# Two chained transformer blocks: context loads and their norm moved within the start, a root fewer in one norm, the last product in column halves

## The chip, the cores and the metric

The kernel runs on one core of a Trainium2 chip. The metric is the device time of one execution in microseconds (us); the time before is a median of three runs. The engines are called TensorE (PE in the rows; PEld is its weight loading), VectorE (DVE), ScalarE (ACT), GpSimd (POOL) and SyncE (SP). SP issues every DMA of this kernel, in one queue.

## The reference, cut to what matters

All tensors are float32. `x` is 256 tokens of 1024 features; `ctx` and `mem` are 256 tokens each. Two blocks run one after the other, depth 1 each.

```
mod   = silu(c) @ w_ada + b_ada;   mod_c = silu(c_ctx) @ w_ada + b_ada     # 6 x 1024 each
h  = rms(x,   g_norm1) * (1 + sc1)  + sh1        # "modulation"
hc = rms(ctx, g_norm1) * (1 + scc1) + shc1
... = split(h @ w_in);  ... = split(hc @ w_in)   # latent attention + retention, both with rotary angles
x  = x + gt1 * ([o_mla, o_ret] @ w_out)
x  = x + gt2 * conv_ffn(rms(x, g_norm2) * (1 + sc2) + sh2)
x  = rms(x, g_final)                             # end of block 1
u  = rms(x, g_mix_pre)                           # start of block 2
z  = u @ w_in_2  -> qa ka va | qh fh ih gh
ya = sliding-window attention(qa, ka, va);  yh = rms(hgrn2(qh, fh, ih), g) * silu(gh)
x  = x + rms([ya, yh] @ w_out_2, g_mix_post)
x  = x + rms(cross_attention(rms(x), rms(mem) @ wk, rms(mem) @ wv) @ wo, g_x_post)
x  = x + rms((silu(u @ w_gate) * (u @ w_up)) @ w_down, g_ffn_post)     # w_down is 2816 x 1024
```

Every rms divides by sqrt(mean of squares + 1e-6).

## The kernel before, in words

Every large product is made of three matmuls (`mm3`, L183): each operand is split into a rounded high part and a low part, and high times high, high times low and low times high are summed in PSUM. A weight arrives as a raw tile of 128 x 1024 (512 KB, one DMA); seven such tiles circulate. ACT writes the high part (L219, or L224 with a gain), DVE the low part (L220, L225), into one of four pairs, more from block 1's feed-forward on. A raw tile is free for the next DMA when its last reader is done.

The program is written as one sequence, and a planner puts it in order: it takes each instruction's place in the text as its priority (a helper with `prio` gets a place some instructions further ahead: 20 for `norm_T`), reckons times with costs of its own, and gives an idle engine the ready instruction of the best place. What comes out is one fixed order for each engine's queue, and an engine works its queue strictly in that order. An instruction far down the text may therefore stand early in a queue.

**The start** is driven by a string, `START`, one letter for each step. `m` is one of 16 steps of the memory's keys and values (`mem_steps`: `k_step` for `wk_x`, `v_step` for `wv_x`; L397 and L183), which need nothing of the modulation; `a` loads one of 16 tiles of `w_ada` and multiplies it straight from the raw tile (`ada_unit`, DMA at L329, matmuls at L331); `x` and `c` load `x` and `ctx` transposed (two DMAs of 512 KB each, L305); `k` loads the rotary constants (258 KB, L450); `X` and `C` call `norm_T` on the one or the other. `norm_T` squares on ACT (L360), adds on DVE (L362 to L365), sums over features with two matmuls against a column of ones (L368), takes the root on POOL (L136, L137), spreads it with a matmul (L375, L377) and multiplies the tile (L430). After the last `a`, `ada_fm` turns the two sums into columns (copy L336, transposes L343, L346, L350), `mod_split` modulates `x` on ACT and DVE (L471, L474) and splits it (L157, L158), and the memory steps that are left follow (L483). Then comes the first product of block 1 (`proj`, the retention's queries), in whose course `mod_split` runs for `ctx`, and the product for the latent attention's inputs, the first to read `ctx`.

**Block 2** works the two halves of the tokens (`seg2(0)` and `seg2(1)`) as generators, one some steps behind the other. At its head (L1352 to L1375) block 1's last residual is added, `xr` and `gx = xr * g_final` are squared and summed on ACT (L141), and POOL makes two scalars for each token: `r1`, the root of the final norm, and `r`, that of both norms together. ACT then scales `gx` by `r1` (L1375), and each product of `w_in_2` is scaled by `r` when it leaves PSUM (L1395). `hgrn2` (L1150 to L1208) ends with its own norm: ACT squares the output `o` (L1199), DVE multiplies `o` by the gate (L1201) and reduces the squares (L1203), POOL takes the root, DVE multiplies by it (L1206), and PE transposes the result (`transpose_split`, L165).

**The end** (L1470 to L1472) is the last six rows of tiles of `w_down`, six units for each half of the tokens; each unit multiplies into two PSUM tiles of 512 columns. `post_norm` follows for each half: squares on ACT (L141), gain on DVE (L1090), root on POOL (L145, L146), scaled addition on DVE (L1095), DMAs out.

Of the kernel before, what the change touches and what calls it, by code (L numbers as in the profile page):

```python
# [14 lines left out]
ALU = mybir.AluOpType  # L15
AX = mybir.AxisListType
# [4 lines left out]
D = 1024  # L21
KD = D // P
FF = 2816
KF = FF // P
EPS = 1e-6
# [5 lines left out]
MLA_ACT = (2, 5)  # L31
MOD = 'VVAVVAVA'
MID = 1
START = 'mmaamxXmaammaammaamaamaakmaaacaC'
NT2 = 5
NS1 = 4
ZORD = ('ka', 'qa', 'qh', 'gh', 'fh', 'ih')
# [50 lines left out]
def _body(nc, tc, A, out, es):  # L88
# [202 lines left out]
    with ExitStack() as e1:  # L291
# [133 lines left out]
        @prio("nt")  # L425
        def norm_T(dst):
            r, rb = token_rms(dst)
            for q in range(2):
                ks = slice(4 * q, 4 * q + 4)
                nc.vector.tensor_tensor(out=dst[:, ks, :], in0=dst[:, ks, :],  # L430
                                        in1=rb.unsqueeze(1).broadcast_to([P, 4, T]), op=ALU.mult)

        n_mem = n_ada = 0
        for ch in START:
            if ch == "m":
                mem_steps[n_mem]()
                n_mem += 1
                if n_mem == 2:
                    mem_norm()
            elif ch == "a":  # L440
                ada_unit(1 - n_ada % 2, n_ada // 2, ada0[1 - n_ada % 2])
                n_ada += 1
            elif ch == "x":
                for q in range(2):
                    load_T(xnT, "xT", q)
            elif ch == "c":
                for q in range(2):
                    load_T(cnT, "ctxT", q)
            elif ch == "k":
                nc.sync.dma_start(c1, A["cst1"][:, 128:NC1])  # L450
            elif ch == "X":
                norm_T(xnT)
            elif ch == "C":
                norm_T(cnT)
        while n_ada < 16:
            ada_unit(1 - n_ada % 2, n_ada // 2, ada0[1 - n_ada % 2])
            n_ada += 1
# [22 lines left out]
            return X  # L480

        hx = mod_split(xnT, sh1[:, 0:8], sc1[:, 0:8])
        for i in range(n_mem, 16):  # L483
            mem_steps[i]()

        rdec = cp.tile([P, 8], F32, name="rdec")
        bc_row(rdec, "ret_decay")
# [514 lines left out]
        split_from(hh[:, 0:nb, :], hl[:, 0:nb, :], ya[:, 0:nb, :])  # L1002
        return hh, hl

    def ffn_down(u, t, hT, accs):
        k = u.ks[0]
        hh, hl = hT[k // 4]
        sl = slice(t * P, (t + 1) * P)
        wh, wl = u.get()
        mm3(accs, hh[:, k % 4, sl], hl[:, k % 4, sl], [wh[:, 0:512], wh[:, 512:1024]],  # L1010
            [wl[:, 0:512], wl[:, 512:1024]], k == 0, k == KF - 1)

    wdown_units = units_for(W, A["w_down"], 0, 1024, KF)
    bcs = {}
# [134 lines left out]
    @prio("h2")  # L1149
    def hgrn2(t, ih, parts, gate):  # L1150
        qs, ks, qi, kd, decs = parts
        Sst = once("state", state)[0]
        at = at_tile()
        for h in range(4):
            for c in range(2):
                cols = slice(h * P + 64 * c, h * P + 64 * c + 64)
                nc.tensor.matmul(at[64 * c:64 * c + 64, cols], lhsT=ks[:, cols], rhs=qs[:, cols], start=True, stop=True)
        for c in range(2):
            cs = slice(64 * c, 64 * c + 64)
            blocks = lambda a: a[cs, :].rearrange("p (h c n) -> p h c n", h=4, c=2)[:, :, c, :]  # L1160
            nc.vector.copy_predicated(blocks(ATs), C2("causal")[cs, cs].bitcast(U32).unsqueeze(1).broadcast_to([64, 4, 64]),
                                      blocks(at))
        tt = tr_tile()
        for h in range(4):
            hs = slice(h * P, (h + 1) * P)
            nc.tensor.transpose(tt[:, hs], kd[:, hs], ident)
        kdT, yh = pair()
        nc.scalar.copy(kdT, tt)
        nc_ = 2 - t
        kvs = [at_tile() for _ in range(nc_)]  # L1170
        for h in range(4):
            hs = slice(h * P, (h + 1) * P)
            for c in range(nc_):
                nc.tensor.matmul(kvs[c][:, hs], lhsT=kdT[64 * c:64 * c + 64, hs], rhs=ih[64 * c:64 * c + 64, hs],
                                 start=True, stop=True)
        for c in range(nc_):
            cg = 2 * t + c
            if cg == 0:
                nc.scalar.copy(Sst[0], kvs[c])
            else:  # L1180
                for h in range(4):
                    hs = slice(h * P, (h + 1) * P)
                    nc.vector.scalar_tensor_tensor(out=Sst[cg][:, hs], in0=Sst[cg - 1][:, hs],
                                                   scalar=decs[:, 2 * h + c:2 * h + c + 1], in1=kvs[c][:, hs],
                                                   op0=ALU.mult, op1=ALU.add)
        o = at_tile()
        for h in range(4):
            hs = slice(h * P, (h + 1) * P)
            for c in range(2):
                cs = slice(64 * c, 64 * c + 64)  # L1190
                nc.tensor.matmul(o[cs, hs], lhsT=ATs[cs, h * P + 64 * c:h * P + 64 * c + 64], rhs=ih[cs, hs],
                                 start=True, stop=2 * t + c == 0)
            for c in range(2):
                cg = 2 * t + c
                if cg:
                    nc.tensor.matmul(o[64 * c:64 * c + 64, hs], lhsT=qi[:, h * P + 64 * c:h * P + 64 * c + 64],
                                     rhs=Sst[cg - 1][:, hs], start=False, stop=True)
        sq = S2()
        nc.scalar.activation(sq, o, AF.Square, scale=128.0 ** -0.5)  # L1199
        if gate is not None:  # L1200
            nc.vector.tensor_tensor(out=yh, in0=o, in1=gate, op=ALU.mult)  # L1201
        ss = small(4, "hss")
        nc.vector.tensor_reduce(out=ss, in_=sq.rearrange("p (h n) -> p h n", h=4), axis=AX.X, op=ALU.add)  # L1203
        r = finish_rstd(ss, 4)
        src = o if gate is None else yh
        nc.vector.tensor_tensor(out=yh.rearrange("p (h n) -> p h n", h=4), in0=src.rearrange("p (h n) -> p h n", h=4),  # L1206
                                in1=r.unsqueeze(2).broadcast_to([P, 4, P]), op=ALU.mult)
        return yh  # L1208
# [137 lines left out]
    def seg2(t):  # L1346
# [17 lines left out]
        for i in range(2):  # L1364
            c = slice(i * 512, (i + 1) * 512)
            nc.vector.tensor_tensor(out=gx[:, c], in0=xr[t][:, c], in1=g[:, c], op=ALU.mult)
            mean_sq(xr[t][:, c], D, ss[0][:, i:i + 1])
            mean_sq(gx[:, c], D, ss[1][:, i:i + 1])
        r1 = rstd2(ss[0])
        r = small(1, "rf")  # L1370
        nc.gpsimd.tensor_tensor(out=r, in0=r1, in1=r1, op=ALU.mult)
        nc.gpsimd.tensor_scalar(out=r, in0=ss[1][:, 0:1], scalar1=ss[1][:, 1:2], scalar2=r, op0=ALU.add, op1=ALU.mult)
        r = finish_rstd(r)
        nc.gpsimd.tensor_tensor(out=r, in0=r, in1=r1, op=ALU.mult)
        nc.scalar.activation(xr[t], gx, AF.Copy, scale=r1)  # L1375
        yield
        Z, zs = {}, []
# [90 lines left out]
                for t in range(2):  # L1468
                    ffn_down(u, t, hT2, dacc[t])
    for t in range(2):  # L1470
        for u in down[16:]:
            ffn_down(u, t, hT2, dacc[t])  # L1472
        post_norm(t, dacc[t], "g_ffn_post", True)


# [83 lines left out]
```

## Time and profile before

| | |
|---|---|
| median of 3 runs | 839.96 us (839.39 to 840.77) |
| profiled execution | 838.46 us, its span 836.7 us |
| mean granted clock of TensorE | 0.992 of full speed |
| busy: PE, PEld, DVE, ACT, POOL | 804.2, 652.2, 618.8, 481.1, 40.7 us |
| DMA | 155.20 MB, 186 GB/s over the span |

Times in rows count from the start of the span. In a timeline, the bracket behind an instruction tells how long its engine stood idle before it and what it waited for. In a table of stretches, each engine's busy time stands with its number of instructions, and the last three columns are the granted clock of TensorE, the busy share of the DMA engines and GB/s.

### The profile page before, as it was taken

The numbers are of one execution on the slowest core, as the hardware profiler recorded it, in microseconds if no ns is written. First come the engines' busy times: TensorE is split into PE (matmuls) and PEld (weight loads), VectorE is DVE, ScalarE is ACT, GpSimd is POOL, SyncE is SP. The second block draws the span as 40 slices with busy tenths as digits, with TensorE's granted clock in tenths as the row PEclk, the third lists the DMA queues.
The fourth block names the chain that finished last, engine by engine and source line by source line (L and its number), as shares of the span: only waits on it lengthen the run. The fifth ranks groups of instructions, "written<-read, shape, count | busy, mean of one in ns | idle before, by whom it ended". The sixth has DMA issues, their size and how long they took to land.

```text
span 836.7 us, 11995 instructions
## 1 busy us (share of the span) xinstructions
PE 804.2 (96%) x4384; PEld 652.2 (78%) x4384; DVE 618.8 (74%) x1043; ACT 481.1 (58%) x850; POOL 40.7 (5%) x76
## 2 busy tenths in 40 slices
PE   5989999999999999999999999999999999999996
PEld 4757978776787888888887777767888788888885
DVE  5739889996787698878868656786747887867743
ACT  7338364334655685656656656565626876756631
POOL 0000010000010200000001300001001100000000
PEclk9999999999999999999999999999999999999999
DMA  9797889872166557566564453343624576566501
GB/s 336 262 359 267 268 288 327 280 232 78 49 186 186 180 186 226 179 200 198 181 177 153 134 166 127 126 130 121 201 76 121 173 240 197 178 200 195 184 1 51
DMA packets 81531, 155.20 MB, mean 186 GB/s; under 512 B 5184, under 2 KB 43584, under 8 KB 81472
## 3 DMA queue, kind: packets, MB, share of 16 engines
q1 hardware_dynamic: 81472, 154.44, 57.4%
q8 instruction: 34, 0.56, 0.3%
q14 instruction: 25, 0.20, 0.1%
HBM read 152.85 MB, written 1.05 MB: 184 GB/s over the span
## 4 chain that ended last, share of the span: by engine, by line
PE 77%; ACT 3%; DVE 2%; POOL 2%; issue 2%; POOLq 0%; DVEq 0%; ACTq 0%
PE acc L183 38%; PE tr L250 9%; PE at L250 7%; PE tr L253 4%; PE at L253 4%; PE at L746 2%; PE tr L768 1%; PE at L183 1%; ACT junk L141 1%; PE tr L165 1%; PE at L1326 1%; PE tr L757 1%; PE at L1304 1%; PE at L718 1%; POOL rs L137 1%
## 5 line engine op out<-in xcount | busy, mean ns | idle before, releaser
L183 PE MATMUL acc<-wh,xT 128*128 128x512 f32 (+2 forms) x544 | 169.3, 388 | 1.8 <-ACT xT L157 1.8
L219 ACT CAST wh<-raw 128x1024 fp32r<-128x1024 f32 (+1 forms) x90 | 91.1, 1012 | 84.1 <-PE acc L183 31.1
L220 DVE TENSOR_TENSOR wl<-raw,wh 128x1024 fp32r<-128x1024 f32 (+1 forms) x90 | 105.6, 1176 | 40.2 <-ACT wh L219 40.0
L183 PEld LDWEIGHTS acc<-wh,xT 128*128 128x128 f32 x544 | 98.4, 189 | 24.6 <-issue 4.1
L220 DVE TENSOR_TENSOR xl<-raw,xh 128x1024 fp32r<-128x1024 f32 x68 | 82.6, 1220 | 29.8 <-ACT xh L219 29.6
L183 PE MATMUL acc<-wl,xT 128*128 128x512 f32 (+2 forms) x272 | 98.4, 387 | 0.0
L224 ACT ACTIVATE wh<-raw,fm 128x256 fp32r<-128x256 f32 (+3 forms) x128 | 70.4, 605 | 44.4 <-DMA raw<-in_wv_x_dram 15.6
L183 PE MATMUL acc<-xh,xT 128*128 128x512 f32 x288 | 92.8, 397 | 0.0
L219 ACT CAST xh<-raw 128x1024 fp32r<-128x1024 f32 x68 | 70.9, 1047 | 35.7 <-PE acc L183 12.1
L225 DVE SCALAR_TENSOR_TENSOR wl<-raw,fm,wh 128x256 fp32r<-128x256 f32 (+3 forms) x128 | 71.8, 609 | 17.3 <-ACT wh L224 17.1
L183 PEld LDWEIGHTS acc<-xh,xT 128*128 128x128 f32 x288 | 53.6, 189 | 11.6 <-issue 0.7
L250 PE MATMUL tr<-xT,wh 128*128 128x512 f32 x192 | 61.2, 398 | 0.0
L183 PEld LDWEIGHTS acc<-wl,xT 128*128 128x128 f32 x272 | 50.3, 189 | 10.3 <-issue 2.5
L183 PE MATMUL acc<-xl,xT 128*128 128x512 f32 x144 | 53.5, 399 | 0.1
L225 DVE SCALAR_TENSOR_TENSOR xl<-raw,fm,xh 128x256 fp32r<-128x256 f32 (+2 forms) x76 | 38.0, 551 | 14.6 <-ACT xh L224 14.6
L224 ACT ACTIVATE xh<-raw,fm 128x256 fp32r<-128x256 f32 (+2 forms) x76 | 37.7, 559 | 18.5 <-PE acc L183 9.8
L183 PE MATMUL acc<-xh,g 128*128 128x512 f32 x160 | 44.1, 389 | 0.0
L253 PEld LDWEIGHTS tr<-xT,wl 128*128 128x128 f32 x192 | 36.1, 188 | 7.9
L250 PE MATMUL at<-xT,xh 128*128 128x512 f32 x128 | 40.2, 395 | 0.0
L250 PE MATMUL at<-xT,wh 128*128 128x512 f32 x128 | 40.2, 395 | 0.0
L250 PE MATMUL tr<-xT,xh 128*128 128x512 f32 x128 | 40.2, 395 | 0.0
L253 PE MATMUL tr<-xT,wl 128*128 128x256 f32 x192 | 38.6, 278 | 0.0
(366 smaller groups left out, 1544.5 us busy)
## 6 DMA issues: line engine op xcount, KB each, us to landing
raw<-in_w_up_dram SPq DMA_DIRECT2D x66, 512.0 KB, 4.3
raw<-in_w_ada_dram SPq DMA_DIRECT2D x48, 512.0 KB, 5.6
raw<-in_w_down_dram SPq DMA_DIRECT2D x44, 512.0 KB, 4.3
raw<-in_w_in_dram SPq DMA_DIRECT2D x38, 512.0 KB, 4.6
raw<-in_w_gate_dram SPq DMA_DIRECT2D x22, 512.0 KB, 4.7
raw<-in_w_out_dram SPq DMA_DIRECT2D x16, 512.0 KB, 3.6
raw<-in_wk_x_dram SPq DMA_DIRECT2D x8, 512.0 KB, 6.0
raw<-in_wv_x_dram SPq DMA_DIRECT2D x8, 512.0 KB, 8.6
```

Of the source, the lines that this page charges most:

```text
L137: nc.gpsimd.tensor_tensor(out=r, in0=r, in1=mhalf[:, 0:w], op=ALU.pow)
L141: nc.scalar.activation(junk[:, 0:a.shape[-1]], a, AF.Square, scale=n ** -0.5, accum_out=ss)
L165: nc.tensor.transpose(t[:, j * P:(j + 1) * P], src[:, (b + j) * P:(b + j + 1) * P], ident)
L183: nc.tensor.matmul(accs[i], lhsT=xl if f == 2 else xh, rhs=wl[i] if f == 1 else wh[i], start=first and f == 0, stop=last and f == 2)
L219: nc.scalar.copy(wh[:, 0:n], raw[:, 0:n])
L220: nc.vector.tensor_tensor(out=wl[:, 0:n], in0=raw[:, 0:n], in1=wh[:, 0:n].bitcast(F32), op=ALU.subtract)
L224: nc.scalar.activation(wh[:, s], raw[:, s], AF.Copy, scale=gains[k])
L225: nc.vector.scalar_tensor_tensor(out=wl[:, s], in0=raw[:, s], scalar=gains[k], in1=wh[:, s].bitcast(F32), op0=ALU.mult, op1=ALU.subtract)
L250: nc.tensor.matmul(a, lhsT=wh[:, o + b * P:o + (b + 1) * P], rhs=both, start=k == 0, stop=False, skip_group_check=True)
L253: nc.tensor.matmul(a[:, T:2 * T], lhsT=wl[:, o + b * P:o + (b + 1) * P], rhs=X.h[:, k, :], start=False, stop=k == 7, skip_group_check=True)
L718: nc.tensor.matmul(a, lhsT=wt[:, j * P:(j + 1) * P], rhs=xt[:, k, :], start=n == 0, stop=n == 5)
L746: nc.tensor.matmul(sc, lhsT=qTa[0:96, h, ts_], rhs=kTa[h // 4][0:96, h % 4, :], start=True, stop=True)
```

## The change

Four places are changed. In the start, the loads of `ctx` and of the rotary constants come earlier in the string, between memory steps: `ctx` goes from behind the 15th `w_ada` tile to behind the 6th, the constants from behind the 12th to behind the 8th. The norm of `ctx` leaves the string and goes behind the modulation of `x` and one more memory step. In `hgrn2` the reduction of the squares is put ahead of the product with the gate. At the head of block 2 the seven POOL instructions become five: `r1` keeps the sum of squares, `r` is a root of one sum, and the product of two roots is gone; the squares of `gx` come behind both squares of `xr`. At the end, the second half of the tokens does all six units for the left 512 columns and then all six for the right ones.

```diff
-START = 'mmaamxXmaammaammaamaamaakmaaacaC'
+START = 'mmaamxXmaammaacmmaakmaamaamaaaa'
+REST = 'mCmmmm'
...
-            elif ch == "C":
-                norm_T(cnT)
...
         hx = mod_split(xnT, sh1[:, 0:8], sc1[:, 0:8])
-        for i in range(n_mem, 16):
-            mem_steps[i]()
+        for ch in REST:
+            if ch == "m":
+                mem_steps[n_mem]()
+                n_mem += 1
+            elif ch == "C":
+                norm_T(cnT)
...
-    def ffn_down(u, t, hT, accs):
+    def ffn_down(u, t, hT, accs, part=(0, 1)):
...
-        mm3(accs, hh[:, k % 4, sl], hl[:, k % 4, sl], [wh[:, 0:512], wh[:, 512:1024]],
-            [wl[:, 0:512], wl[:, 512:1024]], k == 0, k == KF - 1)
+        cols = [slice(512 * i, 512 * i + 512) for i in part]
+        mm3([accs[i] for i in part], hh[:, k % 4, sl], hl[:, k % 4, sl], [wh[:, c] for c in cols],
+            [wl[:, c] for c in cols], k == 0, k == KF - 1)
...
         nc.scalar.activation(sq, o, AF.Square, scale=128.0 ** -0.5)
+        ss = small(4, "hss")
+        red = nc.vector.tensor_reduce(out=ss, in_=sq.rearrange("p (h n) -> p h n", h=4), axis=AX.X, op=ALU.add)
         if gate is not None:
-            nc.vector.tensor_tensor(out=yh, in0=o, in1=gate, op=ALU.mult)
-        ss = small(4, "hss")
-        nc.vector.tensor_reduce(out=ss, in_=sq.rearrange("p (h n) -> p h n", h=4), axis=AX.X, op=ALU.add)
+            with tc.issue_after(red.ins):
+                nc.vector.tensor_tensor(out=yh, in0=o, in1=gate, op=ALU.mult)
...
             mean_sq(xr[t][:, c], D, ss[0][:, i:i + 1])
-            mean_sq(gx[:, c], D, ss[1][:, i:i + 1])
-        r1 = rstd2(ss[0])
+        for i in range(2):
+            mean_sq(gx[:, i * 512:(i + 1) * 512], D, ss[1][:, i:i + 1])
+        r1 = small(1, "rg")
         r = small(1, "rf")
-        nc.gpsimd.tensor_tensor(out=r, in0=r1, in1=r1, op=ALU.mult)
-        nc.gpsimd.tensor_scalar(out=r, in0=ss[1][:, 0:1], scalar1=ss[1][:, 1:2], scalar2=r, op0=ALU.add, op1=ALU.mult)
-        r = finish_rstd(r)
-        nc.gpsimd.tensor_tensor(out=r, in0=r, in1=r1, op=ALU.mult)
+        e = small(1, "ef")
+        nc.gpsimd.tensor_scalar(out=r1, in0=ss[0][:, 0:1], scalar1=ss[0][:, 1:2], scalar2=EPS, op0=ALU.add, op1=ALU.add)
+        nc.gpsimd.tensor_scalar(out=e, in0=r1, scalar1=EPS, scalar2=None, op0=ALU.mult)
+        nc.gpsimd.tensor_scalar(out=r, in0=ss[1][:, 0:1], scalar1=ss[1][:, 1:2], scalar2=e, op0=ALU.add, op1=ALU.add)
+        nc.gpsimd.tensor_tensor(out=r, in0=r, in1=mhalf[:, 0:1], op=ALU.pow)
+        nc.gpsimd.tensor_tensor(out=r1, in0=r1, in1=mhalf[:, 0:1], op=ALU.pow)
...
-        for u in down[16:]:
-            ffn_down(u, t, hT2, dacc[t])
+        for part in ((0, 1),) if t == 0 else ((0,), (1,)):
+            for u in down[16:]:
+                ffn_down(u, t, hT2, dacc[t], part)
```

`issue_after` keeps the product behind the reduction in DVE's queue.

## Rows read from the trace of the kernel before

**Rows 1.** The page's first part: busy us, share of the span, instructions

```profile
PE 804.2 (96%) x4384; PEld 652.2 (78%) x4384; DVE 618.8 (74%) x1043; ACT 481.1 (58%) x850; POOL 40.7 (5%) x76
```

**Rows 2.** Stretches of the start: length, busy us by engine, clock, DMA share, GB/s

```profile
24.00:32.00 8.00, 6.73 (x54) 4.96 (x54) 6.41 (x12) 2.10 (x4) 0.96 (x2) 1.00 0.61 196
36.00:56.00 20.00, 20.00 (x164) 14.74 (x166) 5.53 (x8) 4.01 (x6) 0.00 (x0) 1.00 0.95 332
58.00:66.00 8.00, 6.05 (x22) 3.54 (x23) 4.87 (x9) 4.07 (x8) 1.38 (x2) 0.57 1.04 376
72.00:88.00 16.00, 16.00 (x72) 13.17 (x71) 15.92 (x26) 12.51 (x19) 0.00 (x0) 1.00 0.92 306
88.00:111.00 23.00, 23.00 (x170) 22.26 (x169) 18.93 (x24) 7.97 (x12) 0.00 (x0) 1.00 0.86 297
```

**Rows 3.** Timeline of PE from 58 to 65 us: start, us, instruction, idle before

```profile
58.96 1.08 PE L331 MATMUL at<-raw,silc 128*32 128x256 f32 x8 [2.25 <-DMA raw<-in_w_ada_dram]
...
60.86 1.01 PE L368 MATMUL tr<-ones,s1k 128*128 128x1 f32 x4 [0.82 <-DVE s1k L365]
...
64.19 1.22 PE L377 MATMUL tr<-s1k,ones 128*128 128x256 f32 x2 [0.17 <-DVE s1k L375]
```

**Rows 4.** Timeline of SP's queue in the start

```profile
48.79 0.90 SPq L305 DMA_DIRECT2D s<-in_ctxT_dram  x2
49.78 0.60 SPq L329 DMA_DIRECT2D raw<-in_w_ada_dram  x1
51.92 5.86 SPq L209 DMA_DIRECT2D raw<-in_wv_x_dram  x5
```

**Rows 5.** Timeline of ACT around 57 to 61 us

```profile
57.31 1.06 ACT L360 ACTIVATE g<-s 128x1024 f32<-128x1024 f32 x1 [0.23 <-DMA s<-in_ctxT_dram]
60.47 1.33 ACT L224 ACTIVATE wh<-raw,fm 128x512 fp32r<-128x512 f32 x2 [2.11 <-DMA raw<-in_wv_x_dram]
```

**Rows 6.** All waits of PE: waiting line, releaser, us, times, longest

```profile
PE tr L165 <- DVE g L1206: 2.5, 2, 1.7
...
PE acc L183 <- DVE wl L225: 1.3, 2, 0.8
```

**Rows 7.** Timeline of DVE at 6 us

```profile
5.73 0.16 DVE L1063 TENSOR_TENSOR lmx<-fm 128x4 f32<-128x4 f32 x1 [4.44 <-DMA fm<-in_fm_dram]
```

**Rows 8.** Groups of DVE from 56 to 93 us: count, busy us, mean ns

```profile
L430 DVE TENSOR_TENSOR s<-s,tr 128x1024 f32<-128x1024 f32 x2 | 2.4, 1218 | 0.7 <-PE tr L377 0.7
L362 DVE TENSOR_TENSOR g<-g,g 128x1024 f32<-128x1024 f32 x1 | 1.2, 1226 | 6.2 <-ACT g L360 6.2
```

**Rows 9.** Timeline of DVE in the second half's hgrn2

```profile
565.49 0.69 DVE L1201 TENSOR_TENSOR g<-at,g 128x512 f32<-128x512 f32 x1 [1.47 <-ACT t L1199]
```

**Rows 10.** Two more stretches: behind hgrn2's second norm, and one with short stalls

```profile
570.00:576.00 6.00, 6.00 (x24) 4.75 (x23) 4.63 (x6) 3.60 (x8) 0.87 (x2) 0.72 0.26 87
112.00:117.50 5.50, 3.48 (x16) 1.67 (x15) 3.19 (x14) 4.37 (x17) 2.80 (x6) 1.00 0.89 349
```

**Rows 11.** Timeline of POOL at block 2's head, first and second half of tokens

```profile
459.17 2.49 POOL L1371 TENSOR_TENSOR rf<-rs 128x1 f32<-128x1 f32 x1
...
467.84 0.19 POOL L1371 TENSOR_TENSOR rf<-rs 128x1 f32<-128x1 f32 x1
```

**Rows 12.** Timeline of DVE in the same stretch

```profile
459.79 1.22 DVE L220 TENSOR_TENSOR wl<-raw,wh 128x1024 fp32r<-128x1024 f32 x1
```

**Rows 13.** Timeline of ACT in the same stretch

```profile
459.13 1.16 ACT L1375 ACTIVATE xr<-g,rs 128x1024 f32<-128x1024 f32 x1 [0.77 <-POOL rs L146]
...
464.86 0.48 ACT L1395 ACTIVATE g<-acc,rs 128x256 f32<-128x256 f32 x1 [3.97 <-POOL rs L1374]
```

**Rows 14.** Timeline of PE in the same stretch

```profile
467.81 0.39 PE L183 MATMUL acc<-wh,xT 128*128 128x256 f32 x1 [1.23 <-ACT xT L157]
```

**Rows 15.** Timeline of ACT and PE at the end

```profile
829.22 0.39 PE L183 MATMUL acc<-wh,g 128*128 128x512 f32 x1
...
829.75 0.60 ACT L141 ACTIVATE junk<-acc 128x512 bf16<-128x512 f32 x1
```

More of the change, by code (lines that the diff above doesn't have):

```diff
@@ L482, in _body @@
         hx = mod_split(xnT, sh1[:, 0:8], sc1[:, 0:8])
-        for i in range(n_mem, 16):
-            mem_steps[i]()
+        for ch in REST:
[4 more added lines that the diff above has]
+                norm_T(cnT)
+        assert n_mem == 16
         rdec = cp.tile([P, 8], F32, name="rdec")
```

## The prediction

> **What bounds the kernel now.** The page's first part comes first: PE is busy for 804.2 us of the span, far ahead of DVE's 618.8 [rows 1]. A gain can therefore come from two places only: time in which PE stands still, and time in which it works at the lower of its two clocks. The table of stretches shows where the start loses both. From 36 to 56 us PE is busy for 20.00 of 20.00 us while DVE does 5.53; from 58 to 66 us the granted clock is 0.57, so that most of the stretch runs at 1.2 GHz instead of 2.4; from 72 to 88 us PE and DVE are both full (16.00 and 15.92 of 16.00 us) [rows 2]. PE's timeline then says what stood ahead of the slow stretch: PE waits 2.25 us for the last tile of `w_ada`, then 0.82 us for DVE's sum of ctx's squares, then 0.17 us for ctx's spread root [rows 3]. SP's queue shows why that tile is late: ctx's two loads are issued right ahead of it, at 48.79 us, the tile itself at 49.78, and the DMA engines are 95% busy from 36 to 56 us [rows 2, 4]. Last, the list of PE's waits: of what is behind the start, the wait of hgrn2's transpose for DVE (2.5 us in two waits, the longer 1.7) is touched by the change, and the 1.3 us for low parts of weights may be [rows 6].
>
> **The start.** Removed from the queue ahead of the last w_ada tile are two loads of 512 KB, 1.05 MB; at the 376 GB/s of the slow stretch they take 2.8 us [rows 2, 4]. They don't vanish: ctx now goes ahead of five weight tiles and nine tiles of w_ada, and the constants (258 KB) ahead of two weight tiles and four of w_ada. From 24 to 32 us the DMA engines are busy for 0.61 of the time [rows 2]; the free 3.1 us hold 1.17 MB at 376 GB/s. So ctx fits in and 0.14 MB of the constants are left over, 0.4 us, for the tiles behind. I cost that at nothing, because PE is full from 36 to 56 us and its next tile is there when it asks; without that cover it is the 0.4 us. The first reader of the constants comes far behind their old place.
>
> The last w_ada tile lands 2.8 us sooner, which covers the 2.25 us of waiting. The two waits for ctx's norm (0.82 and 0.17) lie ahead of the first transposes of the modulation and go with the norm: 3.24 us in all [rows 3]. What is late next is the weight of the twelfth memory step: ACT begins its high part at 60.47 us, when its DMA lands [rows 5]. It is behind the same 1.05 MB, so about 57.7; half of ACT's 1.33 us later PE can begin, 58.4. PE is through with the last w_ada tile at 58.96 - 2.25 = 56.7 and half of the row's 1.08 us at the full clock, 57.3 [rows 3]. A new wait of 1.1 us stands in place of the old 3.24.
>
> The clock: 6.05 us of work at 0.57 cost 6.05 x 0.43 = 2.6 us [rows 2]. It fell behind a wait of 2.25 us; a wait of 1.23 us elsewhere is followed by no slow stretch [rows 14], nor are the short stalls from 112 to 117.5 us, where PE works for 3.48 of 5.50 us at clock 1.00 [rows 10]. The new 1.1 us is nearest to these, so I count the 2.6 as won. Sum of the start: 3.24 + 2.6 - 1.1 = 4.7 us. The bounds are 2.1 (the clock falls all the same) and 5.8 (no new wait).
>
> The norm of ctx still issues all it did: two squares on ACT, eight instructions on DVE, three matmuls, two on POOL, whose queue holds nothing else until the norms of the latents, much later. On DVE the two squares' sum (1.2 us) and the multiplication (2.4) are the long ones [rows 8]. They compete with low parts of weights wherever they go, and DVE is full from 72 to 88. Two things cover them: DVE is idle for 14.5 of the 20 us before 56, and the planner does put ready work far ahead of its place in the text, as line 1063, of block 2, which runs at 5.73 us [rows 2, 7]. If that cover is gone, DVE's 23 us from 88 to 111, with 18.93 busy [rows 2], still leave 4.1 for work that comes late. I take nothing, with the 1.3 us of rows 6 unchanged.
>
> **hgrn2.** The product with the gate (0.69 us [rows 9]) stands between the squares and their reduction; behind the reduction it runs beside POOL's root, and the root comes 0.69 us sooner. PE's waits there are 1.7 and 0.8 us [rows 6], both longer, so both shrink: 1.4 us. Behind the longer one follows a stretch at clock 0.72: 6.00 x 0.28 = 1.7 us [rows 10]. With the wait down to about 1.0 us, again nearest to the 1.23 us of rows 14, I count it as won; its ends are 0 and 1.7.
>
> **Second norm.** Seven POOL instructions become five, but `r1` now comes last, behind `r`. In the first half of the tokens POOL's product at L1371 takes 2.49 us, in the second half 0.19 [rows 11]; while the slow one lasted, DVE ran instructions on two SBUF operands such as the 1.22 us of L220 [rows 12]. ACT waits 3.97 us for `r` at L1395, and PE later 1.23 us for ACT [rows 13, 14]. If `r` is sooner and ACT takes L1395 first, PE's 1.23 us are the most that can be won. If ACT's queue has L1375 first, as now, ACT waits for the later `r1`, and L1395 is behind its 1.16 us [rows 13]. Plus 1.2 or minus 1.2, with nothing in the rows to choose by: I take nothing.
>
> The Trainium skill, "SBUF — State Buffer", section "Who interferes with whom", says that a DVE instruction with two SBUF inputs and a GpSimd instruction that reads SBUF exclude each other for the whole instruction. By that rule the pair 2.49 and 0.19 is no accident, POOL's last root is held up by the next DVE run, and the change is worth the minus 1.2; it is a rival below.
>
> **End in halves.** The same 36 matmuls in another order. The second square starts at 829.75, and the last matmul ends at 829.22 + 0.39 = 829.61 [rows 15]; at most 0.14 us can be won, and nothing is added behind. Nothing.
>
> **Sum.** 4.7 + 1.4 + 1.7 = 7.8 us. The profiled execution took 838.46 us (span 836.7 and 1.8 around it), 1.5 below the median of the runs shown, so 830.7 for it and 839.96 - 7.8 = 832.2 for the median.
>
> **Rivals.**
> *The clock falls all the same.* Both stretches keep a wait of about 1 us close behind other short ones, and the one row of a harmless 1.23 us is thin evidence. Then 2.1 + 1.4 = 3.5 us are won: 836.5.
> *The root that comes last.* ACT holds L1375 ahead of L1395 and waits for `r1`, the case of the rule above: 1.2 us lost, 833.4. For it speaks the order of ACT's queue now [rows 13], against it that this depends on the planner's reckoning.
> *PE stands at ctx's sums.* This is the other side. ctx's tiny matmuls hold up all that is queued behind them on PE. If the planner reckons them ready sooner than DVE, full of low parts, makes them, PE waits. The longest wait is the norm's chain from the end of the second square (57.31 + 1.06 = 58.37 [rows 5]) to the spread at 64.19 [rows 3], 5.8 us, and a slow clock behind it costs 2.6 once more. That turns the start's 4.7 into a loss of 3.7; with hgrn2's 1.4, and no more than that, 842.3. It decides against the change once the wait is over 3.5 us (3.5 + 2.6 = 4.7 + 1.4). Against it: now PE waits just 0.82 and 0.17 us there.
> *It doesn't do what it says.* The DMA backlog stays, because a raw tile is asked for again as soon as it is free; the last w_ada tile and the twelfth weight come when they did, and PE, which interleaves the two halves, finds no shorter chain in hgrn2: 839.96 give or take 1.
>
> **How the numbers follow.** Chances: the forecast 0.48, the clock 0.20, the late root 0.08, PE at ctx's sums 0.14, nothing 0.10. A difference of 0.2%, 1.7 us, is about what a measurement of this kernel can tell. The first three are faster by more: 0.76; nothing is the same: 0.10; PE at ctx's sums is slower: 0.14. The lower end is 839.96 - 5.8 - 1.4 - 1.7 - 1.2 = 829.9, with a little for an order of the queues that happens to fall well: 829.4. The upper end takes in the clock and nothing: 840.5, and leaves out PE at ctx's sums.
>
> **What would show it.** In the changed profile the wait for w_ada should be gone from PE's list, the clock should be 1.00 from 58 to 66 us, and the twelfth memory step should start near 58.4; hgrn2's two waits should be near 1.0 and 0.1 us, with clock 1.00 behind. A new long wait of PE at L368 or L377, a slow stretch anywhere in the first 70 us, or ACT standing longer ahead of L1395 would prove the matching step wrong. Above 838 us the start's sum has failed.

## The result, and the profile after

The changed kernel takes 834.53 us (median of 4 runs, 833.53 to 835.03) against 839.94 before (4 runs); ratio 0.9943, 95% interval 0.9924 to 0.9962. By the medians that is 5.4 us faster, by the ratio 4.8 (3.2 to 6.4); 832.2 was forecast, within a range of 829.4 to 840.5. Every ratio here is the one on record, with the few much slower executions left out, and need not be the quotient of the two medians beside it. The profiled execution of the kernel after took 835.03 us (span 833.3), that of before 838.46 (836.7): the two profiles differ by 3.4 us only, so the profiles show less of the gain than the medians do. In the changed file most lines sit one or a few numbers lower: L183 became L184, L224 L225, L377 L378, L331 L332.

The first part of the page of after (busy us, share, instructions). Set against [rows 1], the work is nearly the same: PE is busy 0.7 us less, and POOL has four instructions fewer.

```profile
PE 803.5 (96%) x4384; PEld 652.5 (78%) x4384; DVE 618.6 (74%) x1043; ACT 481.7 (58%) x850; POOL 40.5 (5%) x72
```

Stretches of after (length, busy us by engine with counts, clock, DMA share, GB/s):

```profile
24.00:32.00 8.00, 6.74 (x53) 4.74 (x52) 6.40 (x12) 3.70 (x6) 0.96 (x2) 1.00 0.87 312
36.00:56.00 20.00, 20.00 (x150) 14.47 (x148) 7.49 (x12) 4.01 (x6) 0.00 (x0) 1.00 0.88 282
58.00:66.00 8.00, 3.89 (x21) 2.47 (x21) 5.49 (x18) 6.14 (x11) 0.93 (x2) 0.87 1.02 375
64.00:70.00 6.00, 5.78 (x13) 3.88 (x14) 6.00 (x7) 4.24 (x8) 0.00 (x0) 0.50 0.62 204
570.00:576.00 6.00, 6.00 (x29) 4.98 (x28) 4.24 (x6) 2.04 (x4) 0.87 (x2) 1.00 0.59 177
```

Beside [rows 2, 10], the loads went into the free room of 24 to 32 us, as forecast (196 GB/s there before, 312 now). But from 36 to 56 us the rate fell from 332 to 282 GB/s. 50 GB/s over 20 us are 1.0 MB, about the 1.05 MB taken out of that stretch: the transfers behind did not move up, the queue moved less. From 58 to 66 us PE now works for 3.89 us instead of 6.05, and the slow clock has only wandered, to 64 to 70 us. The slow stretch at 570 us is gone.

SP's queue in the start of after (start, us, instruction); then what SP waits for from 20 to 62 us (line, releaser, us in all, times, longest), after and before:

```profile
21.51 0.90 SPq L306 DMA_DIRECT2D s<-in_ctxT_dram  x2
...
46.02 4.16 SPq L330 DMA_DIRECT2D raw<-in_w_ada_dram  x4
52.90 4.87 SPq L210 DMA_DIRECT2D raw<-in_wv_x_dram  x5
```

```profile
SPq L330 <- PE at L332: 9.6, 3, 3.9
SPq L210 <- PE at L332: 8.4, 5, 3.0
SPq L330 <- DVE wl L226: 5.0, 3, 2.6
```

```profile
SPq L209 <- PE at L331: 10.5, 6, 3.0
SPq L329 <- DVE wl L225: 7.2, 4, 2.6
SPq L329 <- PE at L331: 4.9, 2, 3.0
```

This is why the rate fell. SP stands 23.0 us for a reader to free a raw tile (PE at a w_ada tile, DVE at a low part), and 22.6 before: in both kernels the readers set when the next tile is asked for. The twelfth step's weight, the first of the five at 52.90, was issued at 51.92 before [rows 4]. The DMA view gives the us from issue to landing in its last column, before and after:

```profile
raw<-in_wv_x_dram SPq DMA_DIRECT2D x1, 512.0 KB, 8.4
```

```profile
raw<-in_wv_x_dram SPq DMA_DIRECT2D x1, 512.0 KB, 7.2
```

So the weight lands at 60.1, where it landed at 60.3. It comes no sooner.

PE's timeline of after, ACT's and DVE's beside it (start, us, instruction, idle before and what ended it):

```profile
58.18 0.44 PE L344 MATMUL tr<-ident,s1k 128*128 128x128 f32 x2 [0.49 <-ACT s1k L337]
...
59.95 0.50 PE L369 MATMUL tr<-ones,s1k 128*128 128x1 f32 x4
63.89 1.19 PE L378 MATMUL tr<-s1k,ones 128*128 128x256 f32 x2 [3.44 <-DVE s1k L376]
64.52 0.99 PE L184 MATMUL acc<-wh,s 128*128 128x512 f32 x1
```

```profile
60.35 1.58 ACT L470 ACTIVATE s<-s,sh,sc 128x256 f32<-128x256 f32 x3 [0.73 <-DVE sh L347]
61.84 1.97 ACT L158 CAST xT<-s 128x1024 fp32r<-128x1024 f32 x2
63.72 1.94 ACT L225 ACTIVATE wh<-raw,fm 128x512 fp32r<-128x512 f32 x3
```

```profile
60.35 1.70 DVE L473 TENSOR_SCALAR s<-s,sc,sh 128x256 f32<-128x256 f32 x5
61.98 0.15 DVE L371 COPY ss<-tr 128x2 f32<-128x2 f32 x1
63.26 0.48 DVE L376 TENSOR_SCALAR s1k<-ident,rs 128x128 f32<-128x128 f32 x2 [1.14 <-POOL rs L138]
```

The wait for w_ada and ctx's 0.82 us [rows 3] are gone. PE now stands for 0.49 us at each of the two columns' copies, which the forecast did not count, and for 3.44 us at ctx's spread root, whose sum DVE copies (L371) only behind five pieces of x's modulation. A second thing is late at the same time, and this wait covers it: the twelfth weight, landed at 60.1, is converted by ACT (L225) at 63.72 only, since ACT first does three pieces of the modulation (L470) and two of its casts (L158). The experiments tell the two apart. In all, PE stands as long as before; the stretch from 56 to 84 us, before and after, has 4.54 and 4.64 us without PE's work:

```profile
56.00:84.00 28.00, 23.46 (x110) 16.77 (x101) 22.87 (x46) 22.03 (x34) 1.38 (x2) 0.88 0.85 291
```

```profile
56.00:84.00 28.00, 23.36 (x115) 17.26 (x114) 22.59 (x45) 20.34 (x32) 0.93 (x2) 0.88 0.85 291
```

PE's list of waits, after (compare [rows 6]; waiting line, releaser, us, times, longest):

```profile
PE tr L166 <- DVE g L1212: 1.3, 2, 0.9
...
PE tr L344 <- ACT s1k L337: 1.0, 2, 0.5
```

Block 2's head, POOL and ACT of after (columns as above; compare [rows 11, 13]):

```profile
459.15 1.57 POOL L1383 TENSOR_TENSOR rg<-rg,mhalf 128x1 f32<-128x1 f32 x1
460.72 2.69 POOL L1381 TENSOR_SCALAR rf<-ss,ef 128x1 f32<-128x1 f32 x1
463.49 0.57 POOL L1382 TENSOR_TENSOR rf<-rf,mhalf 128x1 f32<-128x1 f32 x1
...
466.94 0.56 POOL L1383 TENSOR_TENSOR rg<-rg,mhalf 128x1 f32<-128x1 f32 x1
470.48 0.38 POOL L1381 TENSOR_SCALAR rf<-ss,ef 128x1 f32<-128x1 f32 x1 [2.98 <-ACT junk L142]
```

```profile
460.75 1.15 ACT L1384 ACTIVATE xr<-g,rg 128x1024 f32<-128x1024 f32 x1 [0.77 <-POOL rg L1383]
...
464.10 0.48 ACT L1404 ACTIVATE g<-acc,rf 128x256 f32<-128x256 f32 x1 [1.58 <-POOL rf L1382]
```

`r1`'s root (L1383) stands last in the text, yet the planner put it ahead of `r`'s sum (L1381). So L1384 waits 0.77 us, as before, and L1404 waits 1.58 us instead of 3.97. Part of that difference is only that ACT comes to L1404 later; e3 below tells how much sooner the eviction is. PE's waits of 1.23 and 0.3 us there are down to one of 0.2.

Where the time came from is seen when the start of the same instruction of PE, counted from the first, is compared in the two traces. PE is 0.2 us behind at its first matmul, 1.1 behind at 77 us, 1.6 behind from 118 to 460 us, 0.5 ahead at 471, 1.7 ahead at 570, 3.3 ahead at 584, and stays there. So the start lost 1.4, the norm won 2.1, hgrn2 with the slow stretch behind it 2.8, the end nothing. These are of two executions only.

### The profile page after: what moved, and what is told of

It is laid out like the page before. It is cut to its first block, busy times and chain, and to the rows that moved or that the text cites. A ratio compares the mean times of both kernels' runs of the same rounds, so it can differ in the third digit from the quotient of the medians.

```text
span 833.3 us, 11985 instructions
## 1 busy us (share of the span) xinstructions
PE 803.5 (96%) x4384; PEld 652.5 (78%) x4384; DVE 618.6 (74%) x1043; ACT 481.7 (58%) x850; POOL 40.5 (5%) x72
## 3 DMA queue, kind: packets, MB, share of 16 engines
q1 hardware_dynamic: 81472, 154.44, 57.7%
HBM read 152.85 MB, written 1.05 MB: 185 GB/s over the span
## 4 chain that ended last, share of the span: by engine, by line
PE 79%; ACT 3%; DVE 2%; issue 1%; POOL 1%; DVEq 0%; POOLq 0%; ACTq 0%
PE acc L184 40%; PE tr L251 9%; PE at L251 7%; PE tr L254 4%; PE at L254 4%; PE at L750 2%; PE tr L772 1%; PE at L184 1%; PE tr L166 1%; PE at L1332 1%; PE tr L761 1%; PE at L1310 1%; ACT junk L142 1%; PE at L722 1%; POOL rs L138 1%
## 5 line engine op out<-in xcount | busy, mean ns | idle before, releaser
L184 PE MATMUL acc<-wh,xT 128*128 128x512 f32 (+2 forms) x544 | 168.6, 387 | 0.6 <-ACT xT L158 0.5
L184 PEld LDWEIGHTS acc<-wh,xT 128*128 128x128 f32 x544 | 98.0, 188 | 22.9 <-issue 4.1
L184 PE MATMUL acc<-wl,xT 128*128 128x512 f32 (+2 forms) x272 | 97.6, 385 | 0.0
L184 PE MATMUL acc<-xh,xT 128*128 128x512 f32 x288 | 92.6, 397 | 0.0
L225 ACT ACTIVATE wh<-raw,fm 128x256 fp32r<-128x256 f32 (+3 forms) x128 | 70.1, 605 | 37.0 <-DMA raw<-in_wv_x_dram 13.9
L184 PEld LDWEIGHTS acc<-xh,xT 128*128 128x128 f32 x288 | 53.4, 188 | 11.6 <-issue 0.7
L184 PEld LDWEIGHTS acc<-wl,xT 128*128 128x128 f32 x272 | 50.0, 188 | 10.2 <-issue 2.4
L184 PE MATMUL acc<-xl,xT 128*128 128x512 f32 x144 | 53.2, 395 | 0.1
L225 ACT ACTIVATE xh<-raw,fm 128x256 fp32r<-128x256 f32 (+2 forms) x76 | 37.8, 564 | 17.7 <-PE acc L184 9.1
L184 PE MATMUL acc<-xh,g 128*128 128x512 f32 x160 | 44.9, 389 | 0.0
```

Source lines behind the costliest of these rows:

```text
L184: nc.tensor.matmul(accs[i], lhsT=xl if f == 2 else xh, rhs=wl[i] if f == 1 else wh[i], start=first and f == 0, stop=last and f == 2)
L225: nc.scalar.activation(wh[:, s], raw[:, s], AF.Copy, scale=gains[k])
```

## The experiments

Each was timed beside the kernel before on the same chip, in four sessions. The four parts alone come first (before: median 839.06).

**e1, the start alone.** Before with `START`, `REST` and their two loops as changed.

```
-START = 'mmaamxXmaammaammaamaamaakmaaacaC'
+START = 'mmaamxXmaammaacmmaakmaamaamaaaa'
+REST = 'mCmmmm'
...
```

> The kernel before with the start's part of the change alone: early loads, ctx's norm behind x's modulation. Theory A (PE stands in its queue at ctx's spread root, as the changed profile shows with a wait of 3.44 us and clock 0.50 behind it): this part costs what PE is behind after the start there, 1.6 us: 841.5 us against 839.9. Rival, the forecast's sum: it wins 4.7 us, 835.2, and the loss seen in the changed profile comes from another part.

838.74 us, ratio 0.9998 (0.9983 to 1.0013): nothing won. The wait at the spread root is there with the start alone:

```profile
PE tr L378 <- DVE s1k L376: 3.8, 2, 3.4
```

**e2, hgrn2 alone.** Before with the product behind the reduction.

```
-            nc.vector.tensor_tensor(out=yh, in0=o, in1=gate, op=ALU.mult)
...
-        nc.vector.tensor_reduce(out=ss, in_=sq.rearrange("p (h n) -> p h n", h=4), axis=AX.X, op=ALU.add)
+        red = nc.vector.tensor_reduce(out=ss, in_=sq.rearrange("p (h n) -> p h n", h=4), axis=AX.X, op=ALU.add)
+        if gate is not None:
+            with tc.issue_after(red.ins):
+                nc.vector.tensor_tensor(out=yh, in0=o, in1=gate, op=ALU.mult)
```

> The kernel before with hgrn2's part alone. Theory A (both waits of PE for the normed output shrink, and with the longer one below about 1 us the slow stretch behind it goes): 0.4 + 0.8 + 1.6 = 2.8 us won, 837.1, clock 1.00 from 566 to 576 us. Rival (the slow stretch of before has another cause than this wait): 1.2 us won, 838.7, and the clock still falls near 571.

836.25 us, 0.9975 (0.9959 to 0.9991). PE's two waits are 1.3 us together (0.9 the longer) instead of 2.5, and nothing slow follows.

**e3, the second norm alone.** Before with the five POOL instructions of `r1` and `r` in place of the seven.

```
-        r1 = rstd2(ss[0])
...
+        nc.gpsimd.tensor_scalar(out=e, in0=r1, scalar1=EPS, scalar2=None, op0=ALU.mult)
+        nc.gpsimd.tensor_scalar(out=r, in0=ss[1][:, 0:1], scalar1=ss[1][:, 1:2], scalar2=e, op0=ALU.add, op1=ALU.add)
+        nc.gpsimd.tensor_tensor(out=r, in0=r, in1=mhalf[:, 0:1], op=ALU.pow)
+        nc.gpsimd.tensor_tensor(out=r1, in0=r1, in1=mhalf[:, 0:1], op=ALU.pow)
```

> The kernel before with the second norm's part alone. Theory A (one POOL instruction fewer ahead of r and the planner puts r1's root ahead of r's sum, so ACT waits less and PE's 1.23 and 0.34 us go): 2.1 us won, 837.8. Rival (the forecast: the late r1 takes back what r wins): 839.9, or up to 1.2 more.

835.94 us, 0.9960 (0.9945 to 0.9976), the largest of the four. POOL runs in the same order as in the kernel after, and ACT's wait for `r` is 1.58 us here too. As this kernel has the start of before, the times can be compared: ACT begins the eviction at 462.68, 2.2 us sooner than at 464.86 before [rows 13], and PE's lead over before grows by 2.2 us there.

```profile
462.68 0.47 ACT L1398 ACTIVATE g<-acc,rf 128x256 f32<-128x256 f32 x1 [1.58 <-POOL rf L1376]
```

**e4, the end alone.** Before with `ffn_down` given a `part`, and the last product done in two column halves.

```
-        for u in down[16:]:
-            ffn_down(u, t, hT2, dacc[t])
+        for part in ((0, 1),) if t == 0 else ((0,), (1,)):
+            for u in down[16:]:
+                ffn_down(u, t, hT2, dacc[t], part)
```

> The kernel before with the end's column halves alone. All theories: nothing to win but 0.1 us, 839.8; if it is more than 0.5 either way, the order of the last queues was read wrongly.

839.12 us, 0.9993 (0.9974 to 1.0011): nothing that can be measured. In the kernel after, the second square starts 0.10 us behind the last matmul's end; before, it was 0.14 [rows 15].

The medians of the four are 0.3, 2.8 and 3.1 us lower and 0.1 higher, 6.2 won in sum against the 5.4 of the whole change. Within the intervals they add up.

The second session (before: 840.16) takes the start apart.

**e5, early loads with the norm where it was.** Before with the loads moved, ctx's norm still the last of the string.

```
-START = 'mmaamxXmaammaammaamaamaakmaaacaC'
+START = 'mmaamxXmaammaacmmaakmaamaamaaaaC'
```

> The kernel before with the early loads alone; ctx's norm stays in the string ahead of the modulation's columns. Theory A (the loss of the start comes from where the norm stands, not from the loads): PE meets ctx's two tiny matmuls before 50 us, the wait for w_ada and the slow clock are gone, and the start wins about what was forecast, 4.5 us: 835.4. Rival (the loads themselves are what hurts, by standing ahead of weights): no gain or a loss, 840 to 842.

841.09 us, 1.0017 (1.0000 to 1.0034), rather slower. ctx's sums no longer hold PE, but the twelfth weight does, for longer:

```profile
PE acc L183 <- ACT wh L224: 4.4, 1, 4.4
```

**e6, the norm behind the modulation with the loads where they were.**

```
-START = 'mmaamxXmaammaammaamaamaakmaaacaC'
+START = 'mmaamxXmaammaammaamaamaakmaaaca'
...
-        for i in range(n_mem, 16):
-            mem_steps[i]()
+        for ch in 'mCmmmm':
```

> The kernel before with the loads where they were and only ctx's norm moved behind x's modulation. Theory A (the norm behind the modulation leaves PE standing at the spread root, and w_ada is late as before): PE waits 2.25 us for w_ada and some us at the spread root, slower by 1 to 4 us: 841 to 844. Rival (moving the norm is what helps, since the modulation no longer waits behind it): faster by 1 us and more, under 839.

839.24 us, 0.9995 (0.9977 to 1.0012). PE waits 1.0 us for w_ada and 1.4 us at L368: nothing won either.

**e7, the whole change with the norm back ahead of the modulation.**

```
-START = 'mmaamxXmaammaacmmaakmaamaamaaaa'
-REST = 'mCmmmm'
+START = 'mmaamxXmaammaacmmaakmaamaamaaaaC'
+REST = 'mmmmm'
...
+            elif ch == "C":
+                norm_T(cnT)
```

> The changed kernel with ctx's norm put back into the string, behind the last w_ada tile and ahead of the modulation's columns; all else as changed. Theory A: the start's 4.7 us come on top of what the other parts win; by PE's lead 1.6 lost becomes 4.5 won, 834.5 - 6.1 = 828.4. Rival (DVE, full from 72 us on, takes the gain back before 112 us): 831 to 834.

836.47 us, 0.9951 (0.9934 to 0.9969). This fells the theory that ctx's spread root sets the pace of the start. The root is early now, and PE stands 4.39 us all the same. It stands for the twelfth weight, which was issued at 53.73, landed 6.8 us later, at 60.5, and is converted from 66.67 on. PE, then ACT, of this kernel:

```profile
67.45 2.02 PE L184 MATMUL acc<-wh,s 128*128 128x512 f32 x3 [4.39 <-ACT wh L225]
```

```profile
63.30 1.59 ACT L472 ACTIVATE s<-s,sh,sc 128x256 f32<-128x256 f32 x3 [0.73 <-DVE sh L347]
64.79 1.98 ACT L158 CAST xT<-s 128x1024 fp32r<-128x1024 f32 x2
66.67 1.95 ACT L225 ACTIVATE wh<-raw,fm 128x512 fp32r<-128x512 f32 x3
```

**e8, own tiles for ctx's norm.** After, with ctx's norm taking its scratch tile from a buffer of its own and its PSUM tile from those of the products, so that its matmuls need not keep the text's order among the users of the buffers that it shared with the modulation's columns.

```
+            S1 = (lambda: s.tile([P, 256], F32, tag="s1c", name="s1c", bufs=2)) if own else S1_
+            tr_tile = acc_tile if own else tr_
...
-            r, rb = token_rms(dst)
+            r, rb = token_rms(dst, dst is cnT)
```

> The changed kernel with ctx's norm left behind x's modulation in the text, but its small tile and its PSUM tile taken from buffers of their own (a separate tag of two, and the product's accumulators), so that they don't wait for the modulation's columns, which stand ahead in the text on the same buffers. Theory A (the shared buffers, given out in the order of the text, kept the norm late): the norm goes early in the queues and the time is that of the kernel with the norm put back, 828.4. Rival (its place in the text by itself keeps it late): 834.5 as changed.

836.36 us, 0.9958 (0.9941 to 0.9975). ctx's matmuls move up in PE's queue, and the same wait of 4.4 us for `wh` stands in their place. That is the second hit on the spread root theory.

The third session (before: 838.46) moves memory steps ahead of x's modulation in the text, so that ACT converts their weights behind one piece of the modulation.

**e9 and e10, one and two steps ahead.** e7 with one or two `m` more at the end of `START` and as many fewer in `REST`; the diff is that of e9 against e7.

```
-START = 'mmaamxXmaammaacmmaakmaamaamaaaaC'
-REST = 'mmmmm'
+START = 'mmaamxXmaammaacmmaakmaamaamaaaaCm'
+REST = 'mmmm'
```

> e7_back (the whole change, with ctx's norm back in the string ahead of x's modulation) with the twelfth memory step's text also ahead of x's modulation, so that ScalarE converts its weight behind one copy of the modulation (L470/L472) and not behind all of it. Theory B, that PE stands because the modulation is in front of that weight in ScalarE's queue: e7_back's wait of 4.4 us at the twelfth step falls to 1.5 to 2.2 us, but the sums' eviction (L419) then stands behind the rest of the modulation and the thirteenth weight behind that, so a second wait of 2 to 3 us comes at the thirteenth step; the start is at most 1.5 us better than e7_back: ratio to before 0.993 to 0.996. Rival A, that the early norm itself delays PE: no change of the waits, 0.995. Rival D, that PE can have nothing before a transfer that lands late: the wait at the twelfth step names a DMA and stays over 3 us.

> As e9_one_ahead with two memory steps, the twelfth and thirteenth, ahead of x's modulation in the text. ScalarE then converts both weights behind one copy of the modulation; the two steps hold PE for about 5.6 us, longer than the 4 us that the rest of the modulation takes on ScalarE. Theory B: PE waits 1.5 to 2.2 us once, the granted clock of the 70th microsecond is at full speed again, and PE is 3 to 5 us ahead of e7_back at 112 us: ratio to before 0.989 to 0.992. Rival C, that the modulation only moves the wait on: the waits between 60 and 80 us add up to 4 us or more again and the ratio is 0.994 to 0.996. Rival E, given back later: PE is ahead at 112 us but not at 490 us.

e9 834.62 us, 0.9949 (0.9932 to 0.9966); e10 833.18 us, 0.9939 (0.9917 to 0.9961). In e9 the wait is split, 1.5 us at the twelfth step, as expected, and 1.8 at the thirteenth, where 2 to 3 were. In e10 it is one wait of 1.5 us:

```profile
PE acc L184 <- ACT wh L225: 1.5, 1, 1.5
```

So the order in ACT's queue made the wait. In time, e10 fell short of what was expected (0.989 to 0.992): its interval overlaps that of e7.

**e11, the kernel after with one step ahead.** Only the twelfth step's `m` goes ahead of the norm and the modulation.

```
-START = 'mmaamxXmaammaacmmaakmaamaamaaaa'
-REST = 'mCmmmm'
+START = 'mmaamxXmaammaacmmaakmaamaamaaaam'
+REST = 'Cmmmm'
```

> The whole change with ctx's norm behind x's modulation as it is there, and only the twelfth memory step's text ahead of both. The spread root's matmul (L378) then stands behind the first two matmuls of the step in PE's queue. Theory B: the wait of 3.4 us at ctx's spread root falls to 1.5 to 2.2 us at the twelfth weight, and up to 2.5 us more come at the spread root or the thirteenth weight; ratio to before 0.991 to 0.9945. Rival A, that ctx's spread root itself sets the pace: the 3.4 us stay, 0.994 to 0.996.

833.13 us, 0.9939 (0.9916 to 0.9962), the best median of all and ahead of before; against the kernel after (0.9943) the intervals can't separate it. The profiled span is 829.9 us. ACT, then PE, and the table of the two stretches:

```profile
60.51 0.60 ACT L470 ACTIVATE s<-s,sh,sc 128x256 f32<-128x256 f32 x1 [0.73 <-DVE sh L347]
61.02 1.32 ACT L225 ACTIVATE wh<-raw,fm 128x512 fp32r<-128x512 f32 x2
```

```profile
61.77 1.03 PE L184 MATMUL acc<-wh,s 128*128 128x512 f32 x2 [1.16 <-ACT wh L225]
62.69 1.19 PE L378 MATMUL tr<-s1k,ones 128*128 128x256 f32 x2
```

```profile
60.00:64.00 4.00, 2.84 (x11) 1.75 (x11) 2.98 (x10) 2.87 (x5) 1.04 (x2) 0.75 1.04 389
64.00:70.00 6.00, 4.79 (x17) 3.14 (x17) 6.00 (x9) 5.11 (x9) 0.00 (x0) 0.88 0.63 228
```

PE starts the twelfth step at 61.77 instead of 64.52, and the spread root behind it waits for nothing. The loss at the slow clock, 1 minus the granted clock times the length of the stretch, is 4.00 x 0.25 + 6.00 x 0.12 = 1.7 us; in the kernel after it was 3.4 between 56 and 84 us.

**e12, the start alone with one step ahead.** e1 with the same two strings as e11.

> Before with the start part alone (as e1_start, which gave 0.9998 and a wait of 3.4 us at ctx's spread root) and with the twelfth memory step's text ahead of ctx's norm and of x's modulation. This is the forecast's start term without what failed in it. Theory B: the 3.4 us wait is 1.0 to 1.5 us at the twelfth weight, the granted clock between 64 and 72 us is above 0.75, PE is 1 to 3 us ahead of before at 118 us, and the ratio is 0.995 to 0.998. Forecast as it stood (4.7 us won): 0.994 to 0.995. Rival E, that the start wins nothing whatever PE does there, since block 2's head takes it back: PE ahead at 118 us, not at 490 us, ratio 0.999 to 1.001.

In the fourth session, 838.79 us against 839.29, ratio 1.0002 (0.9986 to 1.0019). The wait of 3.4 us is 1.2 us here and at the twelfth weight, as expected, but no time is won: at 118 us PE is 0.7 us better placed against before than at its first matmul, where 1 to 3 were expected, and by the interval at most 0.14%, 1.2 us, can be hidden in the timing. PE works for 24.18 of the 28 us from 56 to 84, 0.7 more than before: most of the standing came back in other places. So the longest wait in the start is explained. What the start could give at best is not: with this order it is about nothing, and the 4.7 us of the forecast lie outside the interval.

```profile
56.00:84.00 28.00, 24.18 (x119) 16.75 (x118) 22.12 (x45) 20.43 (x32) 1.04 (x2) 0.94 0.82 291
```

## Why the prediction was right in sum and wrong in its parts

The range held the time, and its sign was right. The composition was not: where 4.7, 3.1, 0 and 0 us were forecast, the parts alone measured 0.3, 2.8, 3.1 and nothing. That the time fell into the range is luck in part: the norm's 3.1 us, taken at nothing, stood in for the start's 4.7.

**The start failed, at the step "It is behind the same 1.05 MB, so about 57.7".** The forecast took the queue to be short of bandwidth. It was short of free tiles: SP's issue of the twelfth weight waits for PE to read w_ada, and the 1.0 MB show up as a lower rate. The weight landed at 60.1. The rival "It doesn't do what it says" named this mechanism (a raw tile is asked for again as soon as it is free) and had 0.10; for the twelfth weight it was the true one. The last w_ada tile, which PE awaited before, did come early enough: that wait went.

**The next step failed too: "What is late next is the weight of the twelfth memory step ... A new wait of 1.1 us".** The right tile, but the wrong cause and size. What came is the prediction's own sign of a wrong step, a new long wait of PE at L377 (L378 after). [rows 5] show ACT idle for 2.11 us ahead of that weight, so its transfer was counted as the only thing it waits for. Once w_ada is on time, x's modulation is ready first and stands ahead of the weight in ACT's queue, as it does in the text: 3.4 us in the kernel after, 4.4 in e5, e7 and e8, 1.2 to 1.5 once the step is ahead of it (e9 to e12). The rival "PE stands at ctx's sums" saw a long wait in the right place; its owner was only half right, since taking ctx's sums out of the way gave a longer wait.

**The clock's 2.6 us were not won.** From 56 to 84 us the profiles of e2, e3 and e10 to e12 each lost 1.7 us to the granted clock, all the others, before and after among them, 3.4 (over the whole stretch; the forecast's 2.6 counted PE's busy time alone). e2 and e3 have before's start unchanged, so the same code loses the one or the other. The reason given for winning it, that a wait of about 1.2 us is followed by no slow stretch, did not hold either: e11 and e12 wait 1.2 us there and the clock falls, and in e1 and e5 it falls right behind the very wait that was called harmless [rows 14]. This is the rival "The clock falls all the same", which had 0.20. e1:

```profile
460.00:500.00 40.00, 38.03 (x209) 30.64 (x207) 23.39 (x38) 24.67 (x51) 8.45 (x17) 0.96 0.49 145
```

**hgrn2 was right in its mechanism and its size.** The waits shrank from 2.5 to 1.3 us, with 1.4 forecast. The 1.7 us of the slow stretch are not the fixed cost of the wait that the prediction booked: e1, e3 and e4 keep the waits of 2.5 us, and their clock at 564 to 576 us is 1.00. They are not without a tie to it either: of the seven profiles with the old waits four have the slow stretch (before, e5, e6, e12), of the seven with the short ones none.

e4 here; before's line for the same stretch is below it:

```profile
564.00:576.00 12.00, 10.18 (x53) 7.81 (x52) 9.52 (x13) 6.94 (x11) 2.14 (x4) 1.00 0.33 97
```

```profile
564.00:576.00 12.00, 10.19 (x48) 7.62 (x47) 8.28 (x12) 6.81 (x11) 2.14 (x4) 0.86 0.26 87
```

**The second norm was mis-sized: 0 taken, 2 to 3 measured.** The prediction had plus 1.2 or minus 1.2 and "nothing in the rows to choose by". The planner chose the good order: POOL's root of `r1` and the sum for `r` take as long in the first half as the root and the product did before (1.57 and 2.69 us, 1.56 and 2.49), but behind the sum one root of 0.57 us is left of four instructions that took 2.8 in all. Both of PE's waits behind ACT went, 1.5 us, with the chance of a slow stretch behind them: two of the seven profiles that keep those waits (e1 and e5) lose 1.6 us to the clock between 460 and 500 us, and none of the seven with the new norm does. The bound of 1.2 took the longest wait alone.

The cost of the rival "The root that comes last", 1.2 us, did not come. POOL was held up while DVE ran on two SBUF operands, at the root (1.57 us, 0.56 in the second half) as well as at the sum (2.69, and 0.38 with DVE idle), but the root had been held as long before and cost nothing new. The root at 459.15 ends 0.42 us behind a DVE run that ends at 460.30; the sum at 460.72 ends 0.18 us behind a row of such runs that ends at 463.23, the longest of them this:

```profile
461.42 1.22 DVE L221 TENSOR_TENSOR wl<-raw,wh 128x1024 fp32r<-128x1024 f32 x1
```

This agrees with what the Trainium skill, "SBUF — State Buffer", section "Who interferes with whom", says of such a pair, that they exclude each other for the whole instruction.

**The end was right:** nothing.

How far the clock's chance reaches can be read from the timed runs, each of which lists its span and mean granted clock. 1 minus the clock, times the span, is on average 6.8 us for 33 runs of before in the first session, 5.9 for e2, 5.4 for e3, 6.5 for e1 and 6.6 for e4. So of e2's 2.4 us (mean) some 1.0 are clock and 1.4 work; of e3's 3.3, 1.4 and 1.9; e1 and e4 have 0.3 of clock and no work. The clock is listed to 0.001, which is 0.8 us in one run, so these are rough. The forecast for hgrn2, work 1.4 and clock 1.7, is borne out as an average, the clock at some 1.0, and not as the cost of one wait in every execution.

What stays open: why e12, whose profile has a shorter wait and 1.7 us less at the slow clock in the start than that of before, is timed like before; and which of the many short waits lets the clock fall in one execution and not in the next.

## What to carry to other kernels

Before counting megabytes over bandwidth, read what the issuer of the DMAs waits for: here it waited for free tiles, and the bytes taken out of a busy stretch were worth no time. When a wait is removed, look in the text and in each engine's queue for what becomes ready first and stands ahead of the next thing PE needs; here it was the work that the removed wait had held back. A slow stretch of the clock in one profile is a chance that goes with the wait ahead of it and not its fixed cost, and one wait without a slow stretch does not make that wait harmless: see in how many executions of the same code it stands before it goes into a sum.

## What the runs showed of the hardware

In these profiles the falls of the granted clock to 1.2 GHz cost 1.7 us or twice that, at the same few places behind PE's waits (the start, block 2's head, 570 us), the shortest of which was 1.2 us with two of 0.5 just ahead (e11), and they differ between executions of the same instructions. Over 33 runs of before in the first session the time goes with them: 837.75 us on average at a mean clock of 0.994 (9 runs), 838.93 at 0.992 (13), 840.33 at 0.990 (7); the other four, at 0.988 and 0.995, lie further out on either side. The 2.6 us between the first and the last of these groups are as much as a part of this change won. The same POOL instruction on 128 x 1 elements took 2.69 us while DVE ran on two SBUF operands and 0.38 with DVE idle.
